# Which units count as ready in the weight stream of the experts: only the split ones

## The chip, the cores and the metric

The kernel runs on one core of a Trainium2 chip. The metric is the device time of one execution in microseconds (us). The engines are TensorE (PE, matmuls; PEld is its weight load), VectorE (DVE), ScalarE (ACT), GpSimd (POOL) and SyncE (SP), which here issues the loads of the weights from memory to on-chip buffers.

## The reference, cut to what matters

The program is two layers of a hybrid backbone over 256 tokens of width 1024, with 256 context tokens. Layer 0 ends in a dense SwiGLU, layer 1 in a mixture of 8 SwiGLU experts of width 3584, of which each token takes two. The change shows only in that mixture, which holds 352 MB of weights and nearly half of the time:

```python
def swiglu(h, w_gate, w_up, w_down):
    return (jax.nn.silu(h @ w_gate) * (h @ w_up)) @ w_down

def moe_swiglu(h, w_router, b_router, w_gate, w_up, w_down):
    ...
    top_val, top_idx = lax.top_k(logits, TOP_K)
    top_w = jax.nn.softmax(top_val, axis=-1)
    ...
    out = gates[..., 0:1] * swiglu(h, w_gate[0], w_up[0], w_down[0])
    for e in range(1, N_EXPERTS):
        out = out + gates[..., e:e + 1] * swiglu(h, w_gate[e], w_up[e], w_down[e])
    return out
```

All of it is float32.

## The kernel before, in words

**Steps.** An expert gathers its rows with a matmul against a 0/1 matrix and then works through 7 steps of 512 hidden columns. Experts 7, 0, 1 and 2 are *large*: 128 rows (expert 0 has up to 32 more, the *extra rows*). Experts 3 to 6 are *small*: 64 rows. `steps()` (L34) lays the 56 steps out in one order; with B for a large step, X for one of expert 0 and s for a small one it is

```
BBBBsBsBsBsXssXssXssXssXssXssXssBsBsBsBsBsBsBsBsBsBsBBBB
```

**Units.** The weights of a step come as six units of 1 MiB (128 x 2048 float32): two for the gate, two for up, two for down. `experts_units` (L1348) puts them into the stream in the order of use: gate, gate, up, up of the step, then the two down units of the step before. That is 336 units. A unit of a large step is *split*: ScalarE casts a high part `wh` (L104), VectorE subtracts for the low part `wl` (L105), and TensorE makes three matmuls with the parts (`gemm_up` L1803 to L1805, `downs` L1877 to L1879). A unit of a small step is used *whole*, as it lies in its buffer `raw` (`gemm_few` L1816, `downs_few` L1829).

**Buffers and queues.** In this stage there are 9 buffers for raw units and 3 pairs for `wh` and `wl`. `loads()` (L91 to L97) issues a unit's load on SyncE (L96) when the unit nine places before has been taken out of its buffer's slot in the plan; SyncE then waits until that buffer has been read. `one()` takes the next unit in hand: it splits it or notes it as whole. `pump()` (L139) is called at every `next()`, thus each time a unit is used, and takes units in hand until `self.ahead`, here 2, of them are ready. Since every engine works off its own queue in order, the place where `pump()` writes a cast and a subtraction is their place among ScalarE's and VectorE's other instructions.

**One step** (loop in `experts`, L1717 to L1955): the gate's matmuls; `transposes` of the previous step's hidden rows (L1846 for a small step with a copy at L1848, L1851 for a large one, with a cast and a subtraction at L330 and L331); a slot; the up matmuls; a slot; SiLU on ScalarE (L1927); the multiply on VectorE into the hidden rows (L1929); and the down matmuls of the previous step. So a large step's hidden rows, made at its end, are transposed in the middle of the following step, and its down units are used at that step's end. A slot does one piece of the preparation of a later expert: `pick` on VectorE (L1536, L1618 for a small expert, L1654 and L1656 for the extra rows), `gather` on TensorE (L1545, L1627, L1665), `affine` on ScalarE or VectorE (L1592, L1633, L1635), and `back`, which ends with a cast (L1603) and a sum (L1604).

The functions of the stream that the change touches or that call it:

Of the kernel before, what the change touches and what calls it, by code (L numbers as in the profile page):

```python
# [67 lines left out]
class Stream:  # L68
# [70 lines left out]
    def pump(self, n=None):  # L139
        n = self.ahead if n is None else n  # L140
        self.loads()
        while len(self.hl) < n and self.i_do < len(self.items):
            self.one()

    def next(self):
# [1985 lines left out]
```

## Time and profile before

| | |
|---|---|
| three runs: median, lowest, highest | 2049.57, 2048.49, 2050.96 us |
| profiled execution: time, span of the profile | 2049.71, 2048.0 us |
| TensorE busy | 1980.1 us (97%) |
| TensorE weight loads | 1504.0 us (73%) |
| VectorE busy | 1180.0 us (58%) |
| ScalarE busy | 881.8 us (43%) |
| GpSimd busy | 26.7 us (1%) |
| mean granted TensorE clock | 0.989 |
| moved by DMA, mean rate | 517.48 MB, 253 GB/s |

The busy times count executed instructions, so TensorE's 97% leaves about 68 us in which it did nothing; where it waited, and for what, is in the view of waits. The expert stage runs from about 1097 to 2011 us of the span, and its loads are most of the DMA traffic.

### The profile page before, as it was taken

How to read it: one execution, taken by the hardware profiler on the slowest of the kernel's cores; microseconds unless marked ns; L12 is line 12 of the kernel's file. 1: busy time of each engine (PE TensorE's matmuls, PEld its weight loads, DVE VectorE, ACT ScalarE, POOL GpSimd, SP SyncE). 2: the span in 40 equal slices, each digit the busy share in tenths (PEclk: the TensorE clock that was granted, in tenths of full speed). 3: DMA queues.
4: the chain of work that ended last, by engine and by line, in shares of the span. 5: the costliest groups of instructions: out<-in, count | busy, mean ns of one | idle time of the engine just before them, and what ended most of it. 6: DMA issues, size and time to landing. Idle time of an engine off the chain costs nothing. (4 is left out here: it accounts for less than half of the span.)

```text
span 2048.0 us, 29653 instructions
## 1 busy us (share of the span) xinstructions
PE 1980.1 (97%) x11869; PEld 1504.0 (73%) x11869; DVE 1180.0 (58%) x1579; ACT 881.8 (43%) x1208; POOL 26.7 (1%) x36
## 2 busy tenths in 40 slices
PE   8999999999999999899998999999999999999997
PEld 6767888888888888788996776655655566666675
DVE  4755766646876555785566855433333354555486
ACT  6544333244323223665545744422322344454365
POOL 0000000000000000100000000000000000000000
PEclk9999999999999999999999999999999999999999
DMA  7212344433765654233556989999999999999992
GB/s 299 83 54 99 124 154 154 144 114 114 214 199 194 214 176 144 89 105 100 174 181 250 365 333 413 371 377 369 349 387 388 372 392 418 409 417 420 421 420 107
DMA packets 93923, 517.48 MB, mean 253 GB/s; under 512 B 10481, under 2 KB 10737, under 8 KB 50769
## 3 DMA queue, kind: packets, MB, share of 16 engines
q1 hardware_dynamic: 92144, 510.39, 66.4%
q0 software_dynamic: 768, 2.49, 0.4%
q10 hardware_dynamic: 864, 2.62, 0.3%
q8 instruction: 95, 1.56, 0.3%
q14 instruction: 52, 0.42, 0.1%
HBM read 513.36 MB, written 2.10 MB: 252 GB/s over the span
## 5 line engine op out<-in xcount | busy, mean ns | idle before, releaser
L105 DVE TENSOR_TENSOR wl<-raw,wh 128x1024 fp32r<-128x1024 f32 (+1 forms) x364 | 616.7, 1711 | 184.6 <-ACT wh L104 183.9
L104 ACT CAST wh<-raw 128x1024 fp32r<-128x1024 f32 (+1 forms) x364 | 518.0, 1439 | 253.8 <-DMA raw<-in_wfg 77.3
L409 PE MATMUL bka<-hH,wh 128*128 128x512 f32 (+1 forms) x832 | 300.9, 362 | 0.6 <-ACT wh L104 0.6
L411 PE MATMUL bka<-hH,wl 128*128 128x512 f32 (+1 forms) x832 | 294.3, 354 | 1.4 <-DVE wl L105 1.4
L410 PE MATMUL bka<-hL,wh 128*128 128x512 f32 (+1 forms) x832 | 293.8, 353 | 1.5 <-DVE hL L376 1.5
L1816 PE MATMUL bka<-raw,xe 128*64 128x256 f32 x1792 | 205.1, 381 | 1.4 <-DVE xe L1635 1.4
L1805 PE MATMUL bka<-wl,xeH 128*128 128x512 f32 x448 | 178.8, 399 | 4.7 <-DVE wl L105 4.7
L1803 PE MATMUL bka<-wh,xeH 128*128 128x512 f32 x448 | 182.8, 408 | 0.3 <-ACT wh L104 0.3
L1816 PEld LDWEIGHTS bka<-raw,xe 128*64 128x64 f32 x1792 | 124.9, 137 | 77.1 <-issue 18.7
L1804 PE MATMUL bka<-wh,xeL 128*128 128x512 f32 x448 | 177.6, 397 | 0.0
L410 PEld LDWEIGHTS bka<-hL,wh 128*128 128x128 f32 x832 | 157.6, 189 | 26.0 <-issue 2.6
L409 PEld LDWEIGHTS bka<-hH,wh 128*128 128x128 f32 x832 | 157.7, 189 | 25.3 <-issue 2.6
L411 PEld LDWEIGHTS bka<-hH,wl 128*128 128x128 f32 x832 | 157.4, 189 | 23.9 <-DVE wl L105 1.8
L271 DVE SCALAR_TENSOR_TENSOR junk<-raw,silr 128x1024 f32<-128x1024 f32 x128 | 156.3, 1221 | 5.7 <-DMA raw<-in_wmodc 3.9
L1929 DVE TENSOR_TENSOR xf<-xf,bka 128x512 f32<-128x512 f32 (+1 forms) x56 | 30.8, 550 | 153.2 <-PE bka L1805 86.1
L409 PE MATMUL bkd<-hH,wh 128*128 128x256 f32 (+1 forms) x320 | 109.7, 343 | 0.6 <-DVE cx L683 0.6
L411 PE MATMUL bkd<-hH,wl 128*128 128x256 f32 (+1 forms) x320 | 105.8, 331 | 1.0 <-DVE wl L105 1.0
L1803 PEld LDWEIGHTS bka<-wh,xeH 128*128 128x128 f32 x448 | 84.6, 189 | 29.6 <-issue 10.3
L330 ACT CAST htH<-bkt 128x512 fp32r<-128x512 f32 x28 | 16.4, 586 | 208.5 <-PE bkt L1851 208.5
L410 PE MATMUL bkd<-hL,wh 128*128 128x256 f32 (+1 forms) x320 | 105.9, 331 | 0.0
L1805 PEld LDWEIGHTS bka<-wl,xeH 128*128 128x128 f32 x448 | 84.5, 189 | 28.2 <-DVE wl L105 8.2
L1879 PE MATMUL bkd<-wl,htH 128*128 128x512 f32 x224 | 91.5, 408 | 11.3 <-DVE wl L105 11.2
(392 smaller groups left out, 2849.5 us busy)
## 6 DMA issues: line engine op xcount, KB each, us to landing
raw<-in_weg SPq DMA_DIRECT2D x112, 1024.0 KB, 9.3
raw<-in_weu SPq DMA_DIRECT2D x112, 1024.0 KB, 8.8
raw<-in_wed SPq DMA_DIRECT2D x112, 1024.0 KB, 8.9
raw<-in_win SPq DMA_DIRECT2D x92, 512.0 KB, 3.4
raw<-in_wmodc SPq DMA_DIRECT2D x80, 512.0 KB, 4.2
raw<-in_wfg SPq DMA_DIRECT2D x22, 512.0 KB, 3.4
raw<-in_wfu SPq DMA_DIRECT2D x22, 512.0 KB, 4.5
raw<-in_wfd SPq DMA_DIRECT2D x22, 512.0 KB, 4.1
```

Source lines behind the costliest of these rows:

```text
L104: self.nc.scalar.copy(h, t)
L105: self.nc.vector.tensor_sub(l, t, h)
L271: nc.vector.scalar_tensor_tensor(junk, t, 1.0, silr[:, s], op0=OP.mult, op1=OP.mult, accum_out=modc[l][:, v, s, m:m + 1])
L409: nc.tensor.matmul(p, lhsT=lh, rhs=rh, start=first, stop=False)
L410: nc.tensor.matmul(p, lhsT=lh, rhs=rl, start=False, stop=False)
L411: nc.tensor.matmul(p, lhsT=ll, rhs=rh, start=False, stop=last)
L1803: nc.tensor.matmul(p, lhsT=q.xH[:, k], rhs=wh[:, k4], start=(k == 0), stop=False)
L1804: nc.tensor.matmul(p, lhsT=q.xL[:, k], rhs=wh[:, k4], start=False, stop=False)
L1805: nc.tensor.matmul(p, lhsT=q.xH[:, k], rhs=wl[:, k4], start=False, stop=(k == KD - 1))
L1816: nc.tensor.matmul(p[SCAP * g:SCAP * g + SCAP, i * 256:(i + 1) * 256], lhsT=q.x[:, k], rhs=w[:, k4, g * 256:(g + 1) * 256], start=(k == 0) ...
L1879: nc.tensor.matmul(py[c], lhsT=hH_[:, kk], rhs=wl[:, k2, sl], start=False, stop=lst)
L1929: nc.vector.tensor_mul(hid, sg, pu)
```

## The change

`pump()` no longer counts all units in hand, only those whose first entry is not `None`, that is the split ones. While fewer than two split units are ready it goes on taking units, whole ones too, as long as one of those that have been issued is left; it stops before a whole unit when more than five units are in hand. Behind a large step that is followed by a small one, the small step's four whole units are now passed over, and the large step's two down units are cast and subtracted at once.

```diff
--- before.py
+++ after.py
@@ -139,7 +139,12 @@
     def pump(self, n=None):
         n = self.ahead if n is None else n
         self.loads()
-        while len(self.hl) < n and self.i_do < len(self.items):
+        while self.i_do < len(self.items) and len(self.raw) > 0:
+            whole = self.items[self.i_do][2]
+            if sum(u[0] is not None for u in self.hl) >= n and not (whole and not self.hl):
+                break
+            if whole and len(self.hl) > 5:
+                break
             self.one()
 
     def next(self):
```

In the kernel after the change every line behind this place has a number higher by 5 (L1927 is L1932, L1848 is L1853). SyncE's and TensorE's instructions keep their order, as do GpSimd's.

The first place is ScalarE's queue in the late stretch, where large and small steps take turns: `hs` is the copy of a small step's hidden rows, `xf<-bka 128x512` the SiLU of a large step, `128x256` that of a small one, `htH` the cast of the large step's hidden rows. Before:

```order
L1848 COPY hs<-bkt 128x256
L1927 ACTIVATE xf<-bka 128x512
L330 CAST htH<-bkt 128x512
L104 CAST wh<-raw 128x2048 x2
L1927 ACTIVATE xf<-bka 128x256
L104 CAST wh<-raw 128x2048 x4
```

After:

```order
L104 CAST wh<-raw 128x2048 x4
L1853 COPY hs<-bkt 128x256
L104 CAST wh<-raw 128x2048 x2
L1932 ACTIVATE xf<-bka 128x512
L335 CAST htH<-bkt 128x512
L1932 ACTIVATE xf<-bka 128x256
```

The two casts of the large step's down units stood between the cast of its hidden rows and the small step's SiLU; now they stand ahead of the large step's own SiLU.

The second place is VectorE's queue at the pick of the extra rows, in a large step of expert 7: `gs` is the sum in `back`, `rk` and `P` are the pick, `xf<-xf,bka 128x512` is the multiply of a large step. Before:

```order
L331 TENSOR_TENSOR xeL<-xf,xeH 128x512
L105 TENSOR_TENSOR wl<-raw,wh 128x2048 x2
L1604 TENSOR_REDUCE gs<-bkt 128x1
L1654 TENSOR_SCALAR rk_10435<-rank 128x2
L1656 TENSOR_TENSOR P_10136<-iota,rk_10435 128x128 x2
L1929 TENSOR_TENSOR xf<-xf,bka 128x512
L1668 TENSOR_TENSOR xf<-bkt,modc_118 128x256
```

After:

```order
L336 TENSOR_TENSOR xeL<-xf,xeH 128x512
L105 TENSOR_TENSOR wl<-raw,wh 128x2048 x2
L1609 TENSOR_REDUCE gs<-bkt 128x1
L105 TENSOR_TENSOR wl<-raw,wh 128x2048 x2
L1659 TENSOR_SCALAR rk_10455<-rank 128x2
L1661 TENSOR_TENSOR P_10152<-iota,rk_10455 128x128 x2
L1934 TENSOR_TENSOR xf<-xf,bka 128x512
L1673 TENSOR_TENSOR xf<-bkt,modc_118 128x256
```

Two more subtractions, those of the step's down units, now stand ahead of the pick and of the multiply.

## Rows read from the trace of the kernel before

**Rows 1.** Stages: start:end, length, busy of five engines (PE first), PEclk, DMA share, GB/s

```profile
1303.00:1652.00 349.00, 338.57 (x2764) 203.81 (x2757) 119.82 (x100) 105.49 (x118) 0.00 (x0) 1.00 0.95 372
1652.00:1966.00 314.00, 309.36 (x1756) 211.84 (x1757) 168.49 (x117) 141.60 (x120) 0.00 (x0) 1.00 1.01 414
```

**Rows 2.** Waits of TensorE, 1187 to 2012 us: us in total, times, longest

```profile
PE bkd L1879 <- DVE wl L105: 9.6, 15, 0.9
```

**Rows 3.** Waits of TensorE, 1190 to 1663 us

```profile
PE bkd L1879 <- DVE wl L105: 5.1, 8, 0.7
PE bka L1805 <- DVE wl L105: 3.1, 6, 0.6
```

**Rows 4.** Timeline of a late pair: start us, us, engine, operation [idle <-releaser]

```profile
1836.77 2.88 SPq L96 DMA_DIRECT2D raw<-in_wed  x2
...
1841.37 0.60 ACT L1927 ACTIVATE xf<-bka 128x512 f32<-128x512 f32 x1
...
1846.77 0.69 DVE L1929 TENSOR_TENSOR xf<-xf,bka 128x512 f32<-128x512 f32 x1 [4.69 <-PE bka L1805]
...
1853.63 0.66 PE L1851 MATMUL bkt<-ident,xf 128*128 128x128 f32 x4
...
1854.86 3.71 ACT L104 CAST wh<-raw 128x2048 fp32r<-128x2048 f32 x2
...
1856.80 4.49 DVE L105 TENSOR_TENSOR wl<-raw,wh 128x2048 fp32r<-128x2048 f32 x2 [1.11 <-ACT wh L104]
...
1857.83 0.51 PE L1877 MATMUL bkd<-wh,htH 128*128 128x512 f32 x1
...
1861.58 0.39 PE L1877 MATMUL bkd<-wh,htH 128*128 128x512 f32 x1
...
1864.37 0.40 PE L1803 MATMUL bka<-wh,xeH 128*128 128x512 f32 x1
```

**Rows 5.** DMA issues of 1836.5 to 1839.6 us: KB each, median us to landing

```profile
raw<-in_wed SPq DMA_DIRECT2D x2, 1024.0 KB, 12.4
```

**Rows 6.** Timeline behind the third large step, VectorE and TensorE

```profile
1183.05 0.49 DVE L1618 TENSOR_TENSOR P<-iota,rank 128x128 bf16<-128x128 f32 x2
...
1184.51 1.57 PE L1627 MATMUL bkt<-P,xparts 128*128 128x64 bf16 x48
```

**Rows 7.** Timeline at the gather of the extra rows

```profile
1205.73 4.86 SPq L96 DMA_DIRECT2D raw<-in_wed  x2
...
1219.19 1.36 PE L1665 MATMUL bkt<-P,xparts 128*128 128x32 bf16 x48
```

**Rows 8.** DMA issues of 1210.2 to 1210.6 us

```profile
raw<-in_wed SPq DMA_DIRECT2D x1, 1024.0 KB, 7.9
```

**Rows 9.** Timeline at the gather of 1668 us

```profile
1652.37 3.13 SPq L96 DMA_DIRECT2D raw<-in_wed  x2
...
1668.25 1.57 PE L1627 MATMUL bkt<-P,xparts 128*128 128x64 bf16 x48
```

**Rows 10.** DMA issues of 1654.9 to 1655.6 us

```profile
raw<-in_wed SPq DMA_DIRECT2D x1, 1024.0 KB, 11.0
```

**Rows 11.** Timeline at the gather of 1434 us and the next one

```profile
1426.72 4.32 SPq L96 DMA_DIRECT2D raw<-in_weg  x2
...
1436.12 1.50 ACT L1592 ACTIVATE xf<-bkt,modc 128x128 f32<-128x128 f32 x4 [9.02 <-PE bkt L1545]
...
1440.52 1.50 PE L1545 MATMUL bkt<-P,xparts 128*128 128x128 bf16 x24 [0.46 <-ACT hs L1848]
```

**Rows 12.** DMA issues of 1430.6 to 1431 us

```profile
raw<-in_weg SPq DMA_DIRECT2D x1, 1024.0 KB, 7.2
```

**Rows 13.** Timeline of the last pair of steps

```profile
1926.65 2.88 SPq L96 DMA_DIRECT2D raw<-in_wed  x2
...
1943.51 0.66 PE L1851 MATMUL bkt<-ident,xf 128*128 128x128 f32 x4
```

**Rows 14.** DMA issues of 1926.4 to 1929.5 us

```profile
raw<-in_wed SPq DMA_DIRECT2D x2, 1024.0 KB, 12.1
```

## Prediction

> **What bounds the kernel now.** I read the stages first, then TensorE's waits, then one stretch of the timeline with the loads that belong to it. The stage table [rows 1] shows TensorE busy for 338.6 of 349 us and 309.4 of 314 us in the two long stretches of the expert stage, at a granted clock of 1.00, the 2.4 GHz level. The DMA engines are at a share of 0.95 in the first and 1.01 in the second, where they move 414 GB/s. So from 1652 us on both are full: 1.049 MB per unit at 414 GB/s is 2.5 us of load per unit, or 30 us for the twelve units of one large and one small step. SyncE issues a load when the buffer of the unit nine places before it has been read, so TensorE's place sets how far the loads can run ahead.
>
> TensorE's waits in the stage are few. It waits for the low part of a down unit 15 times, 9.6 us in all [rows 2]; before 1663 us there are 8 of these and 6 of the same kind at a gate unit, 5.1 and 3.1 us [rows 3]. The timeline [rows 4] shows where one comes from. The small step's first half ends, TensorE transposes the large step's hidden rows at 1853.63, ScalarE casts them, and only then (1854.86) come the casts of the large step's two down units, and VectorE's subtractions from 1856.80. The matmuls begin at 1857.83 and the first unit takes until 1861.58, 3.75 us, where the next one takes 2.79 (to 1864.37): the stall costs 0.96 us with its restart. The two down units were needed then, and both had long landed: the pair's loads start at 1836.77, the second 2.88 - 0.33 us later at 1839.3, and take 12.4 us [rows 5], so the second is there at 1851.7.
>
> **The change: what it removes.** Units used whole no longer count against the two that are kept ready, so both casts and both subtractions move up past the small units. All stalls of this kind after the first steps should go: 8 x 0.96 + 6 x 0.75 (between its own wait of 0.5 and 0.96) = 12.2 us before 1663 us, and 7 x 0.96 = 6.7 after it. No instruction is added, none is taken away, and SyncE's order of loads stays as it is; the matmuls keep their order too. What moves is the place of two casts on ScalarE and of two subtractions on VectorE, in each of the steps that precede a small one. Both engines work off their instructions in order, so everything that now stands behind them waits with them.
>
> **What it adds, late multiplies.** In the new order the two casts stand before the large step's SiLU, and the two subtractions before its multiply. Now SiLU runs at 1841.37 and the multiply at 1846.77, 6.9 us before the transposes need it [rows 4]. In the new order the second cast cannot start before its unit lands. From there the hidden rows need a cast (half of 3.71), a subtraction (half of 4.49) and the multiply (0.69): 1.9 + 2.3 + 0.7 = 4.9 us. For this pair that is 1851.7 + 4.9 = 1856.6, and the transposes stand ready at 1853.63: a new stall of 3.0 us where one of 0.96 went. That holds as long as TensorE is where it is now against the stream of loads. Once it is later by 3 us, the stall is gone, and the next pairs run without one until TensorE has caught up again: the change makes the kernel need each pair of down units some 8 us sooner.
>
> The Trainium skill says in "DMA: Bandwidth & Descriptors", Rules for kernel authors, to issue a load early and wait for it late; this change moves the wait for the same load ahead, and by that rule it costs. The pair above shows how much: 3.0 against 0.96 us.
>
> **What it adds, late picks and gathers.** At four places other work stands behind the moved instructions. First, after the third large step [rows 6]: VectorE's pick of the next expert's rows runs at 1183.05, at once after the multiply, and TensorE's gather starts at 1184.51, at once after its matmuls. In the new order two subtractions of long landed units (4.5 us) stand between multiply and pick, which then ends at 1183.05 + 4.5 + 0.49 = 1188.1: TensorE waits 3.6 us more. Second, at the pick for the extra rows [rows 7, 8]: the second down unit is issued at 1210.3 and lands 7.9 us later at 1218.2; cast and subtraction give 1222.4, two picking instructions 1223.0; the gather now starts at 1219.19, so 3.8 us more. Third, at 1668.25 [rows 9, 10]: the second unit is issued at 1655.2 and lands at 1666.2, the pick is done 4.7 us later at 1670.9: 2.6 us. Fourth [rows 11, 12]: the scaling of a gathered bank runs at 1436.12 on ScalarE; in the new order it stands behind two casts, the second of a gate unit that lands at 1430.7 + 7.2 = 1437.9 and is cast by 1439.8. The scaling (1.5), a cast (0.6) and the copy that the next gather waits for (0.4) end at 1442.3; that gather starts at 1440.52 now: 1.8 us. Together 11.8 us. Each of these can be less by what the stream of loads gains while TensorE is late; nothing hides them, since the matmuls behind the gather are next on TensorE.
>
> The late multiplies of the ten pairs before 1663 us are bounded by 0 and the 3.0 us of the pair above. The DMA share there is 0.95 against 1.01 [rows 1], so landings come sooner against TensorE than late in the stage; I take 4 us for all ten, nearer to zero than to ten times 3.0, and 0 and 8 as the ends.
>
> **The sum.** Before 1663 us: -12.2 + 11.8 + 4 = +3.6 us. From there on the loads are one full stream, and they take over that delay, because until then they wait for buffers that TensorE frees. What happens in between is given back or taken by the stream, so I go straight to the last pair [rows 13, 14]: its second unit is issued at 1929.2 and lands at 1941.3, the multiply is done 4.9 us later at 1946.2; the transposes stand at 1943.51 now. So TensorE comes out 2.7 us later than the delay of the stream alone, and its last stall of 0.96 us goes: +1.7. Behind that pair there are only large steps and TensorE alone sets the end. In sum +3.6 + 1.7 = +5.3 us on the profiled execution of 2049.7 us, **2055.0 us**; that execution stands 0.1 us above the median of the runs, so the same number holds against it.
>
> Lower bound of the costs: the second pick 0 instead of 3.8, if its unit's load has made up the first delay, and no late multiplies early: 2055.0 - 7.8 = 2047.2. Upper bound: 8 us of late multiplies early, and a restart of 0.4 us (0.96 less a mean wait of 0.6) behind each of about 12 new stalls: 2055.0 + 4 + 4.8 = 2063.8.
>
> **The rivals.** First, **the stalls simply go**: 12.2 + 6.7 = 18.9 us, 2030.8 us. For it: ScalarE is free early (its SiLU runs at 1841.37, the casts only at 1854.86 [rows 4], with one short cast between them in the order), and there is a slack of 6.9 us behind the multiply. Against it: the landings [rows 5, 8, 10, 14] are rows, and no order of instructions can cast a unit before it lands. It decides where a unit lands more than 4.9 us before the transposes; late in the stage that is not so. With the stream full, the 6.7 us of the late stretch cannot come out anyway, so its likelier size is 12.2 us, 2037.5. "Perfetto Trace Analysis", Optimization Strategy, of the Trainium skill would have it so: find the gaps of the busiest engine and make what they wait for start sooner. The gaps of [rows 2] are of this kind, and the rule counts what is freed, not what is put behind it.
>
> Second, **no change within 4 us** (0.2% of 2050 us, about what a measurement of this kernel can tell from none). It comes about if the four places cost half, 6 us in place of 11.8: -12.2 + 6 + 4 + 1.7 = -0.5, 2049.2 us. For it: the loads before 1652 us, at a share of 0.95 [rows 1], leave gaps in which a delay of TensorE lets the stream run ahead. Third, of the same size, **the change does not do what it says**: the split parts have three buffers, and the third is free only when TensorE is through the unit before; then a cast that is earlier in the order starts no earlier. Against that, the multiply at 1846.77 [rows 4] waits for the large step's last matmul, so all three are free by then, eight us before the casts.
>
> Fourth, **the delay spreads**: where TensorE is late its buffers come free late, and in the full stretch each new stall delays the stream once more. If each of the ten late pairs costs the stream 0.8 us, a third of a unit's 2.5 us, that is 8 us more, 2063 us.
>
> **How the numbers follow.** Forecast, slower by more than 4 us within its bounds: 0.50. The spreading delay: 0.07. No change within 4 us, with the third rival: 0.31. Faster, as in the first rival or a part of it: 0.12. That gives 0.12 faster, 0.31 the same, 0.57 slower. The range leaves out the first rival at its full size and the far end of the fourth: 2043 to 2063 us. The forecast's own sum reaches from 2047 to 2064; what of that lies within 4 us of now is counted as no change.
>
> **What the next profile would show.** TensorE's waits for the low part at the down and gate units behind small steps gone, 15 down to one or two. In their place waits of the transposes of the hidden rows for VectorE's multiply in the late pairs, 1 to 3 us each, and of three gathers for the pick. ScalarE's casts of down units waiting for their loads. Loads in the last stretch at the same share and rate. I would be wrong if ScalarE's waits for loads are absent or if the transposes never wait; and wrong in size if the gathers wait less than 2 us each.

## The result, and the profile after

| | before | after |
|---|---|---|
| median of the runs | 2049.03 us (4 runs) | 2092.84 us (4 runs, 2088.44 to 2096.26) |
| ratio | | 1.0215, 95% interval 1.0202 to 1.0227 |
| span of the profiled execution | 2048.0 us | 2086.7 us |

The change makes the kernel 44 us slower, where 5 us were forecast. The profiled execution after the change is the shortest of its four; the two traces differ by 38.7 us, and these are what the traces below account for.

From the page after: the span, the busy times, the group of all casts of weights, and the small gate matmuls (L1821 is L1816 of before):

```profile
span 2086.7 us, 29663 instructions
...
PE 1991.3 (95%) x11869; PEld 1511.6 (72%) x11869; DVE 1184.8 (57%) x1579; ACT 886.7 (42%) x1208; POOL 26.7 (1%) x36
...
L104 ACT CAST wh<-raw 128x1024 fp32r<-128x1024 f32 (+1 forms) x364 | 521.1, 1437 | 462.1 <-DMA raw<-in_wed 132.4
...
L1821 PE MATMUL bka<-raw,xe 128*64 128x256 f32 x1792 | 219.0, 400 | 7.1 <-ACT xf L1932 5.9
```

Two things stand out. ScalarE is idle for 462.1 us ahead of its casts, 253.8 before, and the largest share of that is now waiting for loads of down units. And the small steps' gate matmuls, as many and as large as before, are busy for 219.0 us; before it was 205.1 us.

The two long stretches of the expert stage by the view of windows (start:end, length, busy of PE, PEld, DVE, ACT, POOL, granted clock, DMA share, GB/s), to be held against [rows 1]:

```profile
1340.00:1690.00 350.00, 325.16 (x2572) 196.66 (x2572) 120.85 (x98) 101.20 (x108) 0.00 (x0) 0.97 0.91 355
1690.00:2005.00 315.00, 304.01 (x1719) 208.32 (x1719) 168.19 (x113) 142.17 (x118) 0.00 (x0) 0.98 0.99 404
```

TensorE is busy for 325 of 350 us and 304 of 315. The granted clock is 0.97 and 0.98 where it was 1.00, and the DMA share is 0.91 and 0.99 in place of 0.95 and 1.01: the loads fall back with TensorE, since a load is issued when its buffer has been read, by TensorE or by VectorE's subtraction.

TensorE's waits between 1187 and 2005 us (us in total, times, longest), the eight largest that are new:

```profile
PE bkt L1856 <- DVE xf L1934: 11.5, 7, 2.7
PE bkt L1792 <- ACT hs L1853: 6.4, 1, 6.4
PE bka L1821 <- ACT xf L1932: 5.9, 3, 2.4
PE bkt L1632 <- DVE P L1623: 4.0, 2, 3.1
PE bkt L1851 <- DVE xf L1769: 3.6, 1, 3.6
...
PE bkt L1670 <- DVE P L1661: 2.4, 1, 2.4
PE bkt L1767 <- DVE xf L1769: 2.4, 1, 2.4
PE bkt L1605 <- DVE xe L1638: 1.6, 1, 1.6
```

Both groups of [rows 3] are gone: nothing waits for a weight's low part in this stretch any more. In their place TensorE waits for a multiply (L1934), a SiLU (L1932), a copy of small hidden rows (L1853), a pick (L1623, L1661), a sum (L1769) and an affine step (L1638), all of them work that stands in the queues of ScalarE and VectorE. Why those are late is in ScalarE's own waits in the same stretch:

```profile
ACT wh L104 <- DMA raw<-in_wed: 132.4, 37, 8.4
...
ACT wh L104 <- DMA raw<-in_weg: 62.3, 13, 11.0
```

That is 50 waits, 194.7 us in all. In the trace of before this view has no wait for a load in the expert stage.

**One late pair.** The timeline of the pair whose transposes stall longest (start, length, engine, operation, idle time before it and its releaser), and the loads issued at its head:

```profile
1839.21 3.12 SPq L96 DMA_DIRECT2D raw<-in_wed  x2
...
1851.72 1.90 ACT L104 CAST wh<-raw 128x2048 fp32r<-128x2048 f32 x1 [7.56 <-DMA raw<-in_wed]
...
1854.24 1.90 ACT L104 CAST wh<-raw 128x2048 fp32r<-128x2048 f32 x1 [0.62 <-DMA raw<-in_wed]
1856.05 0.59 ACT L1932 ACTIVATE xf<-bka 128x512 f32<-128x512 f32 x1
1856.17 2.29 DVE L105 TENSOR_TENSOR wl<-raw,wh 128x2048 fp32r<-128x2048 f32 x1 [0.22 <-ACT wh L104]
...
1858.38 0.68 DVE L1934 TENSOR_TENSOR xf<-xf,bka 128x512 f32<-128x512 f32 x1
...
1859.12 0.66 PE L1856 MATMUL bkt<-ident,xf 128*128 128x128 f32 x4 [2.73 <-DVE xf L1934]
...
1859.70 5.36 PE L1821 MATMUL bka<-raw,xe 128*64 128x256 f32 x32
```

```profile
raw<-in_wed SPq DMA_DIRECT2D x2, 1024.0 KB, 12.3
```

The second down unit is issued at 1842.0 (1839.21 + 3.12 - 0.33) and lands 12.1 us later (12.3 above is the median of the two); its cast starts at 1854.24. SiLU stands behind it and runs at 1856.05, though the gate matmuls whose bank it reads ended at 1843.5; the multiply stands behind the second subtraction and runs at 1858.38; the transposes wait 2.73 us. From the landing (1854.1) to the transposes (1859.12) it is 5.0 us, where the prediction had 4.9. Behind the wait the 32 small gate matmuls take 5.36 us, and 3.62 in the half step before it.

**The clock.** The same 32 matmuls of one small step, after a wait of 3.61 us in the changed kernel, and in the kernel before:

```profile
1611.10:1616.40 5.30, 5.30 (x35) 3.15 (x36) 0.69 (x1) 0.00 (x0) 0.00 (x0) 0.67 0.14 29
```

```profile
1592.60:1596.00 3.40, 3.40 (x33) 2.33 (x34) 0.69 (x1) 0.00 (x0) 0.00 (x0) 1.00 1.01 410
```

A mean of 0.67 lies between the chip's two levels, 1.2 and 2.4 GHz, so a part of this stretch ran at 1.2. The price beside the wait is 1.7 us here, and over all of L1821 it is 13.9 us.

**Casts of gates.** The longest delay stands behind casts of gate units. Timeline at 1655 us, at the end of expert 0's last step:

```profile
1659.02 1.90 ACT L104 CAST wh<-raw 128x2048 fp32r<-128x2048 f32 x1 [11.00 <-DMA raw<-in_weg]
...
1661.96 1.90 ACT L104 CAST wh<-raw 128x2048 fp32r<-128x2048 f32 x1 [1.04 <-DMA raw<-in_weg]
1663.76 1.26 ACT L1779 ACTIVATE yH<-bkd,gs 128x512 fp32r<-128x512 f32 x2
...
1665.48 0.38 ACT L1853 COPY hs<-bkt 128x256 f32<-128x256 f32 x1
...
1665.92 0.79 PE L1792 MATMUL bkt<-yH,PT 128*128 128x512 f32 x1 [6.40 <-ACT hs L1853]
...
1669.43 5.23 PE L1821 MATMUL bka<-raw,xe 128*64 128x256 f32 x32
```

Here the next units to split are the gates of the following large step, with six whole units before them. Their casts wait for loads, and the second ends only at 1663.8. The scaling of the finished expert (L1779) and the copy that TensorE needs (L1853) stand behind them; TensorE has nothing to do for 6.40 us before 1665.92, then waits for more of the same chain until the gates of 1669.43. At the place 57 us earlier, the wait of 3.61 us above, it is a sum on VectorE (L1769) that stands behind the subtractions of two gate units.

### The profile page after: what moved, and what is told of

Same layout as the page of the kernel before. It is cut to its first block, busy times and chain, and to the rows that moved or that the text cites. A ratio compares the mean times of both kernels' runs of the same rounds, so it can differ in the third digit from the quotient of the medians.

```text
span 2086.7 us, 29663 instructions
## 1 busy us (share of the span) xinstructions
PE 1991.3 (95%) x11869; PEld 1511.6 (72%) x11869; DVE 1184.8 (57%) x1579; ACT 886.7 (42%) x1208; POOL 26.7 (1%) x36
## 4 chain that ended last, share of the span: by engine, by line
PE 78%; DMA 7%; DVE 6%; ACT 6%; issue 2%; POOL 0%; SPq 0%; ACTq 0%; DVEq 0%
PE bka L1821 9%; PE bka L414 7%; PE bka L416 7%; PE bka L415 7%; DMA raw<-in_wed 6%; PE bkd L414 4%; PE bkd L416 3%; PE bkd L415 3%; PE bka L1808 3%; ACT wh L104 3%; PE bka L1810 3%; PE bka L1809 3%; DVE wl L105 3%; PE bkd L1882 3%; PE bka L1834 2%; PE bkd L1883 2%
## 5 line engine op out<-in xcount | busy, mean ns | idle before, releaser
L104 ACT CAST wh<-raw 128x1024 fp32r<-128x1024 f32 (+1 forms) x364 | 521.1, 1437 | 462.1 <-DMA raw<-in_wed 132.4
L1821 PE MATMUL bka<-raw,xe 128*64 128x256 f32 x1792 | 219.0, 400 | 7.1 <-ACT xf L1932 5.9
L1821 PEld LDWEIGHTS bka<-raw,xe 128*64 128x64 f32 x1792 | 130.8, 144 | 92.0 <-issue 27.4
L1834 PE MATMUL bka<-raw,hs 128*64 128x512 f32 x448 | 102.0, 597 | 0.0
L1809 PEld LDWEIGHTS bka<-wh,xeL 128*128 128x128 f32 x448 | 84.7, 189 | 18.1
L1882 PE MATMUL bkd<-wh,htH 128*128 128x512 f32 x224 | 92.7, 414 | 2.3 <-ACT wh L104 1.6
```

Of the source, the lines that this page charges most:

```text
L104: self.nc.scalar.copy(h, t)
L1809: nc.tensor.matmul(p, lhsT=q.xL[:, k], rhs=wh[:, k4], start=False, stop=False)
L1821: nc.tensor.matmul(p[SCAP * g:SCAP * g + SCAP, i * 256:(i + 1) * 256], lhsT=q.x[:, k], rhs=w[:, k4, g * 256:(g + 1) * 256], start=(k == 0) ...
L1834: nc.tensor.matmul(py[SCAP * c:SCAP * c + SCAP], lhsT=pv["hT"][:, k2, SCAP * h:SCAP * h + SCAP], rhs=w[:, k2, c * 512:c * 512 + 512], star ...
L1882: nc.tensor.matmul(py[c], lhsT=hH_[:, kk], rhs=wh[:, k2, sl], start=fst, stop=False)
```

## The theories, and the experiments

**Theory A**: the new order reaches eight places ahead in a ring of nine buffers: past six whole units (mostly the two down units of the small step before and the four of the next small step's gate and up) to the two that are split. A unit's load has only just been issued when its cast is next in ScalarE's queue. The cast waits for the landing, and everything behind it in that queue, and behind its subtraction on VectorE, waits too. What costs is what stands behind the cast.
**Theory B**: the reach itself costs. Any earlier need pulls TensorE and the loads closer together, whatever stands behind the casts.
**Theory C**: the new order costs without loads, since a long run of casts and subtractions now stands ahead of short urgent work.

Ratios are to the kernel before on the same chip, with 95% intervals.

### How far is passed over

```diff
-            if whole and len(self.hl) > 5:
+            if whole and len(self.hl) > 4:        # run pass4
+            if whole and len(self.hl) > 2:        # run pass2
```

> One unit fewer may be passed over (the break at more than four in hand). The casts of a large step's down units then stand behind that step's SiLU and multiply, and behind the two picks, but still ahead of the small step's gates. Theory A (ScalarE and VectorE stand still behind a cast whose unit has not landed, and what is queued behind the cast makes TensorE late): the transposes no longer wait for the multiply and the gates no longer for SiLU; only the copies of small hidden rows behind the gates' casts stay late, about 10 to 17 us at two places. Time 2045 us (2035 to 2060). Theory B (the reach itself costs, by pulling every need of a unit closer to its load, whatever stands behind the cast): hardly less than with the change, 2080 us or more.

> At most three units in hand when a whole one is taken (the break at more than two). The casts of the down units are placed in the small step's first half, ahead of the cast of the hidden rows, but behind SiLU, multiply and picks of the large step; gates are no longer cast ahead of a copy of small hidden rows. Theory A: nothing that TensorE needs soon stands behind a unit that has not landed, and most of the stalls of before are gone: 2036 us (2028 to 2046). Theory B: between before and the change by reach, about 2060 us.

Measured: pass4 2047.06 us, ratio 0.9994 (0.9984 to 1.0003); pass2 2039.50 us, ratio 0.9953 (0.9937 to 0.9970). Theory A had 2045 and 2036. One unit less in reach takes the whole 44 us away, which theory B does not allow. ScalarE's waits for loads in pass4:

```profile
ACT wh L104 <- DMA raw<-in_wed: 100.0, 31, 10.1
...
ACT wh L104 <- DMA raw<-in_weg: 54.0, 13, 10.3
```

ScalarE still waits 154 us for loads, but SiLU, multiply and the later pick now stand ahead of the casts, and no transposes wait. What is left are the first pick (a wait of 3.1 us, behind two subtractions of landed units), copies behind gate casts, and sums behind subtractions; they eat what the removed stalls give. In pass2 the gate casts go back too, and two kinds of waits of TensorE have grown (before, the first was 2.7 us, and the second was not among them):

```profile
PE bkt L1767 <- DVE htL L336: 5.0, 2, 3.6
PE bkd L1883 <- DVE htL L336: 2.4, 3, 1.2
```

Both are for the low part of the large hidden rows (L336), behind casts that wait for down units.

### Down units alone, gates alone

```diff
+            k = next((i for i in range(self.i_do, len(self.items)) if not self.items[i][2]), None)
+            far = k is not None and (self.items[k][3] == "wed")        # run downs; run gates: != "wed"
+            if not far and len(self.hl) >= n:
+                break
             if sum(u[0] is not None for u in self.hl) >= n and not (whole and not self.hl):
```

> The change for down units alone: whole units are passed over only when the next units to be split are down units; gates keep the rule of before. Theory A: the two longest delays of the trace of the change, 6.1 us at the third small step of expert 5's row and 10.5 us some 55 us later, stood behind casts of gate units; they go, the rest stays: 2093 - 17 = 2076 us (2068 to 2082). Theory B: delays of TensorE are handed on by the stream whatever they come from; 2085 us or more.

> The change for gate and up units alone: whole units are passed over only when the next units to be split are a gate's; down units keep the rule of before. About 15 casts move. Theory A: the two long delays behind gate casts come, and little goes: 2049 + 10 to 17 = 2062 us (2055 to 2068). Theory B: with so few casts moved the stream is pulled no closer, 2050 us.

Measured: downs 2084.89 us, 1.0174 (1.0157 to 1.0191); gates 2061.64 us, 1.0067 (1.0050 to 1.0083). The gates alone cost 14 us, which theory A had in sum. In their trace it is three places with 19 us, the two of theory A and the scaling of 1436 us ([rows 11]), less 5 us of stalls at gate units that are gone. The run of downs is 9 us above theory A's value, outside its range. In its trace the two long delays are gone and other places stall longer: 4.3 us at the gather of the extra rows where it was 2.6, 4.1 at the third pick where it was 1.0, 3.9 at two late pairs where it was 2.8. That trace is of an execution of 2093.49 us, 9 us above the run's median, and the change's trace of one 4 us below its own, so it shows where the delays shift to and not how large they are in the median. That TensorE stalls longer because it is earlier there is argued from this, not tried by itself. By its number, 2085, theory B would do as well here, but not by the two runs before.

### Half of every load

```diff
-            self.nc.sync.dma_start(out=t, in_=self.items[self.i_dma][0])
+            self.nc.sync.dma_start(out=t[:, :1024], in_=self.items[self.i_dma][0][:, :1024])
...
-        self.nc.scalar.copy(h, t)
-        self.nc.vector.tensor_sub(l, t, h)
+        t3 = t[:, None, :1024].to_broadcast([128, 2, 1024])
+        self.nc.scalar.copy(h3, t3)
+        self.nc.vector.tensor_sub(l3, t3, h3)
...
-                        nc.tensor.matmul(..., rhs=w[:, k4, g * 256:(g + 1) * 256], ...)
+                        nc.tensor.matmul(..., rhs=w[:, k4 % 2, g * 256:(g + 1) * 256], ...)
```

> The kernel before, with half of every expert unit loaded (columns 0 to 1023); casts, subtractions and matmuls keep their number and size and read that half twice, so the computation is another and the work on the engines is the same. It is the base for the next run. Theory A and theory B: the stalls of TensorE behind the small steps do not come from loads, so they stay; only the first units of the stage land sooner: 2035 to 2049 us.

> The kernel with the change, half of every expert unit loaded in the same way. Theory A (what stands behind a cast waits for the landing of its unit): units land far ahead, ScalarE no longer waits for loads, the stalls of before are gone, and only the two picks behind subtractions of landed units cost some 3 to 6 us: 10 to 18 us less than the run beside it with half loads. Theory C (the new order itself costs, because long runs of casts and subtractions stand ahead of SiLU, multiplies and copies): some 40 us more than the run beside it, as with full loads.

Measured: before_half 2047.11 us, 0.9997 (0.9987 to 1.0006); after_half 2038.06 us, 0.9953 (0.9935 to 0.9971). With half the loads the change is 9 us faster, with full loads 44 us slower: theory C is out, and the loads are what it hangs on. The stalls of before stay with half loads (TensorE's waits in before_half):

```profile
PE bkd L1888 <- DVE wl L111: 9.7, 15, 0.9
PE bka L1814 <- DVE wl L111: 3.1, 6, 0.6
```

so they never came from loads. With the change they are gone, and ScalarE's waits for loads in after_half are short, 5.0 us at most:

```profile
ACT wh L110 <- DMA raw<-in_wed: 39.9, 18, 3.4
ACT wh L110 <- DMA raw<-in_weg: 39.3, 14, 5.0
```

The gain of 9 is just below the 10 to 18 expected; the first pick alone costs 4.4 us in these two traces.

### Which queue

```diff
+                sg = f2[:, 1]                                      # run silu_early
+                nc.scalar.activation(out=sg, in_=pg, func=AF.Silu)
                 gemm_up(pu, pr, x, px, 1)
...
         self.nc.scalar.copy(h, t)
-        self.nc.vector.tensor_sub(l, t, h)
+        if sum(u[0] is None for u in self.hl) > 5:                 # run sub_late
+            self.late.append((l, t, h))
+        else:
+            self.flush()
+            self.nc.vector.tensor_sub(l, t, h)
...
             nc.vector.tensor_mul(hid, sg, pu)
+            stream.flush()
```

The kernel silu_sub has both.

> The change, with the casts where it puts them, but the subtractions of units that were reached over six whole ones written behind the next multiply (or the next use of a unit). Theory A, ScalarE and VectorE share the cost: SiLU still waits behind casts, but multiply, picks and sums no longer stand behind subtractions, each of which comes 2.3 us after the cast: about half of the loss goes, 2070 us (2060 to 2080). If VectorE alone carries it: 2050 us or less. If ScalarE alone: 2085 us or more.

> The change, with the SiLU of each large step written right behind its gate matmuls, so ahead of the casts that the change puts there; the multiply still stands behind the two subtractions. Theory A with both engines in parallel: the gates that wait for SiLU's bank run on time (9.6 us with their slow matmuls, three places), the transposes still wait for the multiply: 2093 - 10 = 2083 us (2076 to 2088). If ScalarE alone carries the loss: 2060 us or less.

> Both: SiLU ahead of the casts, and the subtractions reached over six whole units behind the multiply. The casts still stand where the change puts them, and wait for loads as long. Theory A: multiply and SiLU are free, so the loss of the down units is gone; the copies of small hidden rows behind gate casts remain. Near the run with the break at more than four: 2050 us (2043 to 2062), much less than the two single runs add up to (11 and some 10 us off 2093). Theory B' (the waits of ScalarE for loads cost by themselves): 2070 us or more.

Measured: sub_late 2081.66 us, 1.0168 (1.0150 to 1.0186); silu_early 2087.67 us, 1.0195 (1.0175 to 1.0215); silu_sub 2057.55 us, 1.0057 (1.0038 to 1.0076). Against the 2092.84 of the change the first gives 11 us and the second 5; both together give 35. By the ratios, each to the kernel before on its own chip, it is 10, 4 and 32; the gain of silu_early alone is not clear of the noise, since its interval overlaps that of the change. The expectation for sub_late, half of the loss, was wrong. With VectorE's queue free the multiply still waits for SiLU, and gates and transposes with it (TensorE's waits in sub_late):

```profile
PE bka L1832 <- ACT xf L1943: 7.5, 4, 2.9
PE bkt L1867 <- DVE xf L1945: 4.7, 4, 1.8
```

The 11 us are net of 3.4 us that TensorE waits in this run for small work of the extra rows (L1701), which now stands behind the moved subtractions. With ScalarE's queue free the multiply still waits for the subtractions, and in silu_early's trace, of an execution 7 us above the run's median, the transposes stall more often than with the change, 12 times:

```profile
PE bkt L1856 <- DVE xf L1937: 17.7, 12, 4.4
```

With both free a late pair runs like this, in the timeline of silu_sub:

```profile
1814.99 0.61 ACT L1941 ACTIVATE xf<-bka 128x512 f32<-128x512 f32 x1
...
1820.39 0.69 DVE L1948 TENSOR_TENSOR xf<-xf,bka 128x512 f32<-128x512 f32 x1 [4.69 <-PE bka L1821]
...
1823.44 1.90 ACT L105 CAST wh<-raw 128x2048 fp32r<-128x2048 f32 x1 [7.84 <-DMA raw<-in_wed]
...
1825.94 1.91 ACT L105 CAST wh<-raw 128x2048 fp32r<-128x2048 f32 x1 [0.61 <-DMA raw<-in_wed]
...
1827.25 0.66 PE L1867 MATMUL bkt<-ident,xf 128*128 128x128 f32 x4
```

SiLU and multiply are early, the casts wait 7.84 us for their loads, and the transposes wait for nothing. ScalarE's waits for loads in silu_sub are even longer than with the change, 218 us:

```profile
ACT wh L105 <- DMA raw<-in_wed: 150.4, 39, 10.2
...
ACT wh L105 <- DMA raw<-in_weg: 67.9, 14, 10.7
```

and the kernel is only 0.57% slower than before; theory B', that these waits cost by themselves, had 2070 us or more. What is left are the first pick (4.5 us), the copy behind the gate casts (7.3, where the change has 10.4), a sum behind subtractions (5.3) and smaller delays, the largest 1.8; together they are more than the removed stalls. A wait of ScalarE for a load costs little by itself.

### One unit ahead in place of two

```diff
-            if sum(u[0] is not None for u in self.hl) >= n and not (whole and not self.hl):
+            if len(self.hl) >= n and sum(u[0] is not None for u in self.hl) >= min(n, 1) and not (whole and not self.hl):
                 break
-            if whole and len(self.hl) > 5:
+            if whole and len(self.hl) > 2:
```

> Two units in hand as before, but at least one of them split; to reach it whole ones are passed over as long as not more than two are in hand. So one down unit is cast ahead of the cast of the hidden rows, the other where it was before. Theory A: the stalls at the down units go and less stands behind late units than with two: the three delays of the run with the break at more than two (6 us together) shrink: 2035 us (2029 to 2042). Theory B: 2040 us or more, since any cast that is placed ahead of need is paid for.

Measured: 2031.86 us, ratio 0.9915 (0.9897 to 0.9933), faster than both kernels; theory B had 2040 us or more. The two long stretches and TensorE's waits in this kernel:

```profile
1303.00:1644.00 341.00, 336.92 (x2748) 205.20 (x2747) 123.83 (x102) 105.66 (x117) 0.00 (x0) 0.99 0.97 382
1644.00:1949.00 305.00, 304.77 (x1745) 210.15 (x1746) 167.74 (x114) 141.26 (x120) 0.00 (x0) 1.00 1.01 416
```

```profile
PE bkt L1767 <- DVE htL L336: 2.7, 2, 1.4
PE bka L1821 <- DVE xe L1640: 1.4, 1, 1.4
PE bkt L1767 <- ACT hs L1853: 0.9, 2, 0.5
```

TensorE is busy for 337 of 341 us and 305 of 305. All the stalls for low parts are gone, in the late stretch too, and the three waits left are of before (2.7, 1.4 and 0.9 us there).

## Why the prediction was right or wrong

The direction was right, and the mechanism for a part: late multiplies and late picks behind casts that wait for landings. The size was wrong by a factor of eight. What failed is the list of what moves and what is made late by it, and the account of the late stretch. The figures here are steps in the time of the first matmul of a unit between the two traces, with the slow matmuls behind a stall included; in sum some 19 us went and 58 came.

- **Removed stalls before 1663 us, -12.2 us**: held. In 14 steps of 0.8 to 1.0 us, 12.1 us.
- **Late picks and gathers, +11.8 us**: about held, 9.5 in all, but not place by place: 5.9 at the first (slow matmuls included), 2.6 and 1.0 at the second and third, nothing at the fourth. TensorE was late there already, as the text had said could be; in the run of gates, where it is not late, the fourth place costs 3.5 us.
- **Late multiplies in the early pairs, +4 us**: the transposes behind them lost 3.1 us. But the step behind it failed: "the place of two casts on ScalarE and of two subtractions on VectorE, in each of the steps that precede a small one" was taken for all that moves, but for one gate unit at the fourth place, and multiply and picks for nearly all that is late. Missed were SiLU itself, whose bank the next gates need (9.6 us at three places), a sum and an affine step on VectorE (4.1 us), and the gates' casts, which also move, over six whole units, ahead of a sum, a scaling and a copy (16.6 us at two places). Together 30 us that stood in no term. The run of gates alone (+14 us) and the runs on the two queues show this part. One of the SiLU places, in the timeline after:

```profile
1369.40 1.90 ACT L104 CAST wh<-raw 128x2048 fp32r<-128x2048 f32 x1 [8.36 <-DMA raw<-in_wed]
...
1371.89 1.90 ACT L104 CAST wh<-raw 128x2048 fp32r<-128x2048 f32 x1 [0.60 <-DMA raw<-in_wed]
...
1373.70 0.59 ACT L1932 ACTIVATE xf<-bka 128x512 f32<-128x512 f32 x1
...
1374.34 5.36 PE L1821 MATMUL bka<-raw,xe 128*64 128x256 f32 x32 [2.38 <-ACT xf L1932]
```

The gates at 1374.34 wait for SiLU, SiLU for a cast, and the cast for a down unit's load.

- **The late stretch, +1.7 us**: failed, it was some 9 us. Removed were 6.9 us of stalls, but six of the ten pairs stalled anew, 15.7 us with the slow matmuls. For a single pair the mechanism was right to 0.1 us (5.0 against 4.9 above), the last pair's transposes wait 2.74 us where the sum had 2.7, and for the pair of [rows 4] the text's own reservation came true: TensorE was late there and did not stall. But "in between is given back or taken by the stream" was wrong. The loads get most of their buffers from TensorE, so they fall back with it, and later pairs stall again. A first down unit of this stretch is used 8.6 to 14.0 us after its landing before, and 11.7 to 16.6 after the change: the new order needs the longer lead, and with the DMA engines at a share of 1 we see no other way for the stream to win it than TensorE being late. No run shows that step by itself.
- **The slow matmuls**: sized at 0.4 us per new stall, for the upper bound only. L1821 alone shows 13.9 us, about 1.7 us for each of the longer stalls.
- **The first rival, "the stalls simply go"**, was argued away for the late stretch by "With the stream full, the 6.7 us of the late stretch cannot come out anyway". The last run refutes it: it gains 17 us, 6 of them in the late stretch with the DMA share at 1.01. The stream had a lead to give, and TensorE used it up: a first down unit is used as little as 4.2 us after its landing there.
- **The fourth rival, "the delay spreads"**, came nearest, but its 2063 us left out the same 30 us and the slow matmuls. The second and the third are out: the order did change, and the time by far more than 4 us.

What the signs for the next profile said came true: the waits for low parts are gone, casts of down units wait for loads, transposes wait 1 to 3 us for the multiply, and gathers for picks.

"DMA: Bandwidth & Descriptors" of the Trainium skill, Rules for kernel authors, has loads waited for late. By that rule the change costs, and the trace agrees, yet the run of silu_sub qualifies it: with 218 us of early waits for loads that kernel is 11 us slower than before and 35 us faster than the change, since less that is urgent stands behind them. What makes such a wait dear is stated in "PSUM — Partial Sum Buffer" of the Trainium skill, Engine vs sequencer instructions: the queues of ScalarE and VectorE are strictly first in, first out. The timeline at 1856.05 shows it, with a SiLU that had been ready for some 12 us.

## What to carry to other kernels

Before work is moved earlier in an engine's queue, list what it is moved past, on each engine, and ask when its input really arrives. A look-ahead nearly as deep as the ring of buffers meets loads that have just been issued, and then it blocks instead of preparing; one unit early enough (here one of two, behind the urgent work of the step) took nearly all the gain. Two queues that block side by side hide each other: freeing one shows little, freeing both shows the cost.

## What had not been expected of the hardware

After single short waits of TensorE its granted clock fell in the small step behind them, at a price of about 1.7 us: so after 1.98 us at 1763, 2.38 us at 1374 and 3.61 us at 1609. After others as long it did not: after 2.40 us at 1226 and 2.35 us at 1427 the clock stayed at 1.00. The length of the wait does not decide it: the same wait of 1.35 us, for the low part of the large hidden rows, stands in the kernel before at 1574 and in lead1 at 1563; behind it the clock stayed at 1.00 before, and in lead1 it was 0.68 for the next 5.3 us, at 1.7 us more for the same 32 matmuls. What tells them apart was not tried. And a stretch whose DMA engines show a share of 1.01 still gave 6 us, out of the lead that its loads had.
